# A two-layer diffusion trunk: two more weight chunks split by DMA and ScalarE, one more chunk by seven products, and sign changes tied to a place

## The chip, the cores and the metric

The kernel runs on one core of a Trainium2 chip. The core has five engines that this document names as the profile does: PE (TensorE, matmuls), DVE (VectorE), ACT (ScalarE), POOL (GpSimd) and SP (SyncE), and 16 DMA engines that serve the queues of all of them. The metric is the time of one execution on the device in microseconds; lower is better.

## The reference

Two layers work on a latent of 512 tokens with 1024 channels. Layer 0 mixes the tokens by attention, layer 1 by a Fourier transform over tokens and channel groups and a linear map. Each layer ends in a gated feed-forward network (FFN) with a convolution of width three over the tokens.

```python
def fourier_mix(h):
    hg = h.reshape(b, l, FNET_GROUPS, d // FNET_GROUPS).astype(F32)
    f = jnp.fft.fft2(hg, axes=(1, 3), norm="ortho").real

def conv_ffn(h, w_up, conv_w, conv_b, w_down):
    u = h @ w_up                                   # 512 x 1024 times 1024 x 5632
    up = jnp.pad(u, ((0, 0), (1, 1), (0, 0)))
    u = up[:, :-2] * conv_w[0] + up[:, 1:-1] * conv_w[1] + up[:, 2:] * conv_w[2] + conv_b
    gate, val = jnp.split(u, 2, axis=-1)
    return (jax.nn.silu(gate) * val) @ w_down

for i in range(DEPTH):
    h = modulate(rms_norm(x, norm_g[i, 0]), sh1, sc1)
    y = attention_mixers(...) if i % 2 == 0 else fourier_mix(h) @ w_f
    x = x + g1 * rms_norm(y, norm_g[i, 1])
    h = modulate(rms_norm(x, norm_g[i, 2]), sh2, sc2)
    x = x + g2 * rms_norm(conv_ffn(h, ...), norm_g[i, 3])
```

## The kernel before

Every large product is made of three matmuls on split numbers: a 32-bit value is a high half that TensorE takes in full and a low half that is what the high half left out. A product is high x high (line 102), low activation x high weight (103) and high activation x low weight (104). A weight thus needs a high half `wh` and a low half `wl`. The usual way (`split`, line 124): an SP DMA loads the raw weight, ACT casts it to `wh`, and DVE subtracts `wh` from the raw weight to give `wl` (both halves show as line 125). The other way (`up_weights_dma`, line 1115): a GpSimd DMA loads the weight straight into the place of the high half, converting as it goes, ACT writes the high half with its sign changed into the place of the low half (line 1121), and a second GpSimd DMA adds the raw weight to it there (line 1124). No DVE instruction is in it. In the code it is a generator in stages, and `pump(g)` lets a generator go on to its next `yield`.

The work runs in this order: modulation vectors and norms at the start, layer 0, the Fourier mixer, the FFN of layer 1 ("second FFN"). A tile scheduler sets the order on each engine's queue; the kernel binds it in places by `fence`/`held` and by dependencies without a semaphore (`add_manual_dep`, NoSync), which only fix who stands ahead of whom in one queue. Each engine works its queue in order.

At the start, `WARM` dummy matmuls (line 638) run on TensorE ahead of the first real work; the sums of the squares of the input (line 184) come next, with more dummies (line 178) between the first modulation products (line 653).

The Fourier mixer ends in an output loop over eight pieces `d` of 128 output channels. A piece's weight comes in raw (`fourier_load` for two pieces into parts of `yT`, others by SP), is turned into a sum (GpSimd, line 1555) and a difference (DVE, line 1556), is split, and is multiplied. The sums stand in `gacc` or in a part of `yT`. In the same loop the weights of the second FFN's first two chunks are made by `up_weights_dma`: four halves `xh`, `xl`, whose stages are let go at d = 1, 4 and 6.

The second FFN goes over 22 chunks `fi`; a chunk is 128 gate and 128 value channels, called its two channels here and numbered u = 2 fi + i. The first three chunks (u = 0 to 5) are begun before their input is complete: five of the six on the two halves of the tokens apart, with the modulation (`remod`, lines 235 to 240) between them. Chunks from 3 on are plain: 48 matmuls of 512 columns, two `wh`/`wl` pairs, of which there are five buffers. The chunks in `SEVEN[1]` are done by a recursive block scheme (Strassen's kind) with seven instead of eight block products: 84 matmuls of 256 columns, and sums of weight blocks (lines 1154 to 1157) that are split in turn; `seven_inputs` prepares the sums of the activations once, ahead of chunk `SUMS[1]`. A chunk's result goes through the convolution (ACT line 1251; DVE lines 1252 and 1254), Silu (ACT 1264), the product (DVE 1265) and a split into `xT` or `xh`/`xl`. The down product of an earlier group of chunks runs in small pieces between the chunks.

The names that the change touches are `WARM`, `SUMS`, `SEVEN`, `up_weights_dma`, `fourier_load`, `fourier_weights`, the output loop, and in `ffn` the choice of a plain chunk's weights:

```python
for i, w in enumerate(up_weights(l, wpair, [fi])):
    ps = mk(pps, [P, T], F32, "mm", 6)
    up_mm(ps, w, slice(0, T))
    cc.append(conv(fi, i, ps))
```

## Time and profile before

| | us |
|---|---|
| runs | 1148.01, 1144.15, 1145.98 |
| median | 1145.98 |
| profiled execution, its own time | 1146.97 |
| its span | 1145.2 |

| engine | busy us | share of the span |
|---|---|---|
| PE | 1113.8 | 97% |
| DVE | 901.1 | 79% |
| ACT | 595.3 | 52% |
| POOL | 173.0 | 15% |

The tables of the profile give times in microseconds from the start of the span. A row of a timeline is: start, duration, engine, line, operation, what it writes from what it reads, shape, count, and in brackets the time that the engine stood idle before it and what it waited for. The share of busy time is a mean over stages; what a change in one stage is worth is read from that stage.

### The profile page before, as it was taken

Reading aid. Unit: us, or ns where it says so; the run is one execution under the profiler, and the core shown is the slowest. Engines: PE = TensorE matmul, PEld = TensorE weight load, DVE = VectorE, ACT = ScalarE, POOL = GpSimd, SP = SyncE. Lnnn points to the kernel's source line nnn. Section 1 sums busy time; section 2 is a strip of 40 time slices with the busy share of each in tenths; the row PEclk is TensorE's granted clock in tenths of the full one; section 3 lists DMA queues with packets and bytes.
Section 4 is the critical chain, followed back from the end, with each engine's and each line's share of the span. In section 5 each row is a group of like instructions: output and inputs, shape, how many; then the busy total and the mean of one; then the engine's idle time right before and its main releaser. Section 6 shows DMA issues by size and latency. Waiting matters only on the chain.

```text
span 1145.2 us, 19542 instructions
## 1 busy us (share of the span) xinstructions
PE 1113.8 (97%) x7796; PEld 966.4 (84%) x7796; DVE 901.1 (79%) x1469; ACT 595.3 (52%) x1068; POOL 173.0 (15%) x180
## 2 busy tenths in 40 slices
PE   8999999999999999999999999899999999999995
PEld 5689988868898978987898898879878898899995
DVE  4678777765679976987999667878998899879755
ACT  4342356666565633552465445557746555555533
POOL 1136332521420000000000143520000000000012
PEclk9999999999999999999999999999999999999998
DMA  9676101075143355635534401822214533323332
GB/s 368 243 241 220 38 1 38 6 262 211 38 185 111 98 200 218 221 120 195 201 106 174 132 5 56 243 107 111 74 47 142 207 102 115 102 79 102 106 143 74
DMA packets 33763, 155.83 MB, mean 136 GB/s; under 512 B 3460, under 2 KB 8196, under 8 KB 22024
## 3 DMA queue, kind: packets, MB, share of 16 engines
q1 hardware_dynamic: 32520, 150.39, 37.0%
q0 software_dynamic: 1152, 4.19, 1.5%
q8 instruction: 61, 1.00, 0.4%
q14 instruction: 30, 0.25, 0.1%
HBM read 148.28 MB, written 6.29 MB: 135 GB/s over the span
## 4 chain that ended last, share of the span: by engine, by line
PE 83%; DVE 9%; ACT 3%; DMA 3%; issue 1%; POOL 1%; DVEq 0%; POOLq 0%; SPq 0%; ACTq 0%
PE mm L102 24%; PE mm L103 22%; PE mm L104 22%; DVE wl L125 2%; PE PT L950 1%; DMA raw<-in_w_up 1%; DVE md_t L302 1%; PE O L102 1%; PE gm L527 1%; PE O L103 1%; PE gm L102 1%; PE mm L178 1%; PE gm L104 1%; PE gm L103 1%; PE O L104 1%
## 5 line engine op out<-in xcount | busy, mean ns | idle before, releaser
L125 ACT CAST wh<-raw 128x1024 fp32r<-128x1024 f32 (+2 forms) x207 | 190.7, 933 | 170.5 <-PE mm L103 115.0
L125 DVE TENSOR_TENSOR wl<-raw,wh 128x1024 fp32r<-128x1024 f32 (+2 forms) x197 | 214.4, 1097 | 53.8 <-ACT wh L125 53.5
L102 PE MATMUL mm<-hh,wh 128*128 128x256 f32 (+1 forms) x632 | 206.4, 327 | 2.1 <-ACT yT L925 0.9
L104 PE MATMUL mm<-hh,wl 128*128 128x256 f32 (+1 forms) x632 | 203.6, 322 | 0.0
L103 PE MATMUL mm<-hl,wh 128*128 128x256 f32 (+1 forms) x632 | 203.5, 322 | 0.0
L277 POOL TENSOR_TENSOR gacc<-gacc,sq 128x256 f32<-128x256 f32 (+1 forms) x33 | 28.0, 848 | 716.6 <-ACT sq L275 715.7
L102 PEld LDWEIGHTS mm<-hh,wh 128*128 128x128 f32 x632 | 118.9, 188 | 18.3 <-ACT sq L1190 5.1
L103 PEld LDWEIGHTS mm<-hl,wh 128*128 128x128 f32 x632 | 118.8, 188 | 11.2
L104 PEld LDWEIGHTS mm<-hh,wl 128*128 128x128 f32 x632 | 118.9, 188 | 10.4 <-DVE wl L125 0.4
L102 PE MATMUL mm<-zh,wh 128*128 128x256 f32 x384 | 109.2, 284 | 0.7 <-ACT sq L1188 0.6
L102 PE MATMUL mm<-xh,wh 128*128 128x512 f32 (+1 forms) x302 | 107.5, 356 | 0.0
L103 PE MATMUL mm<-xl,wh 128*128 128x512 f32 (+1 forms) x302 | 106.8, 354 | 0.0
L103 PE MATMUL mm<-zl,wh 128*128 128x256 f32 x384 | 106.6, 278 | 0.0
L104 PE MATMUL mm<-zh,wl 128*128 128x256 f32 x384 | 106.5, 277 | 0.0
L104 PE MATMUL mm<-xh,wl 128*128 128x512 f32 (+1 forms) x302 | 106.2, 352 | 0.0
L102 PEld LDWEIGHTS mm<-zh,wh 128*128 128x128 f32 x384 | 72.3, 188 | 5.0 <-ACT sq L1193 3.6
L103 PEld LDWEIGHTS mm<-zl,wh 128*128 128x128 f32 x384 | 72.3, 188 | 0.0
L104 PEld LDWEIGHTS mm<-zh,wl 128*128 128x128 f32 x384 | 72.1, 188 | 0.0
L102 PEld LDWEIGHTS mm<-xh,wh 128*128 128x128 f32 x302 | 56.8, 188 | 9.9 <-issue 1.6
L103 PEld LDWEIGHTS mm<-xl,wh 128*128 128x128 f32 x302 | 56.8, 188 | 8.7 <-issue 0.4
L104 PEld LDWEIGHTS mm<-xh,wl 128*128 128x128 f32 x302 | 56.7, 188 | 8.6
L1251 ACT ACTIVATE cv<-mm,cols 128x512 f32<-128x512 f32 x59 | 45.9, 778 | 27.3 <-PE mm L104 21.6
(434 smaller groups left out, 2798.1 us busy)
## 6 DMA issues: line engine op xcount, KB each, us to landing
raw<-in_w_up SPq DMA_DIRECT2D x42, 1024.0 KB, 4.9
xT<-in_mod_r SPq DMA_DIRECT2D x20, 1024.0 KB, 4.9
raw<-in_w_down SPq DMA_DIRECT2D x32, 384.0 KB, 3.1
raw<-in_mod_p SPq DMA_DIRECT2D x8, 1024.0 KB, 4.9
raw<-in_w_down SPq DMA_DIRECT2D x16, 512.0 KB, 4.0
raw<-in_w_in SPq DMA_DIRECT2D x6, 1024.0 KB, 7.7
yT<-in_mod_r SPq DMA_DIRECT2D x10, 512.0 KB, 6.2
raw<-in_w_out SPq DMA_DIRECT2D x4, 1024.0 KB, 4.9
```

The lines of the kernel that those rows point to most:

```text
L102: i = PE.matmul(out, lhsT=ah, rhs=bh, start=start, stop=False, skip_group_check=skip)
L103: PE.matmul(out, lhsT=ah, rhs=bl, start=False, stop=False, skip_group_check=skip)
L104: return i, PE.matmul(out, lhsT=al, rhs=bh, start=False, stop=stop, skip_group_check=skip)
L125: i = S.copy(out=h, in_=src), eng.tensor_tensor(out=l, in0=src, in1=f(h), op=ALU.subtract)
L178: PE.matmul(ps[:32, :src.shape[1]], lhsT=ones32, rhs=src, start=True, stop=True)
L277: G.tensor_tensor(out=self.acc[:, sl], in0=self.acc[:, sl], in1=sq[:, sl], op=ALU.add)
L302: m = V.scalar_tensor_tensor(out=t, in0=yT[:, k, hs], scalar=der[:, l, gi, k:k + 1], in1=R, op0=ALU.mult, op1=ALU.mult)
L527: PE.matmul(ps[32 * q:32 * q + 32, :], lhsT=spad[:, k, :], rhs=w[:, q * T:(q + 1) * T], start=k == 0, stop=k == KC - 1)
L950: PE.transpose(out=pt[:, j * P:(j + 1) * P], in_=Ps[j][:, off:off + P], identity=ident)
L1251: S.activation(out=cv, in_=ps, func=AF.Identity, bias=bc, scale=wc[1])
```

## The change

1. `WARM` goes from 22 to 36.
2. In `up_weights_dma` the sign changes are let go one at a time, each bound behind the ACT instruction that was written last before it; the accumulating DMA of one follows when the next sign change is let go.
3. In the Fourier output loop those stages are let go at d = 1, 3, 4, 5, 6 and 7. The raw weights of pieces 0 and 1 go to other places of `yT` (1 to 3 and 4 to 6), and piece 1's sum to `yT` 2 to 4, so that piece 3's sum no longer shares its place.
4. In the second FFN, chunk 2's weights (`soon`) and chunk 3's (`fourth`) are made by `up_weights_dma` too. The stages of chunk 2 are let go ahead of and between the tiles of the mixer's residual (`rest`), those of chunk 3 before `pre()` and after each `remod`.
5. Chunk 7 joins the chunks that are done by seven products, and their inputs are made ahead of chunk 6.

```diff
--- before.py
+++ after.py
@@ -32,9 +32,9 @@
 
 FIRST = 3
 
-SUMS = [5, 7]
-
-SEVEN = [(5, 6, 8, 10, 12, 14, 15, 17, 18, 20), (8, 9, 10, 11, 12, 13, 14, 15, 16, 17, 18, 19, 20, 21)]
+SUMS = [5, 6]
+
+SEVEN = [(5, 6, 8, 10, 12, 14, 15, 17, 18, 20), (7, 8, 9, 10, 11, 12, 13, 14, 15, 16, 17, 18, 19, 20, 21)]
 
 
 GEMV = {0: (0, 5, 7), 1: (0, 2, 4, 6)}
@@ -50,7 +50,7 @@
 GP = [1, 1]
 BP = [4, 1]
 
-WARM = 22
+WARM = 36
 HOT = [5, 8, 5, 6]
 HOT2 = [2, 2, 2]
 
@@ -1117,11 +1117,15 @@
         for (wh, wl), src in ws:
             G.dma_start(out=wh, in_=src)
         yield
-        for (wh, wl), src in ws:
-            S.activation(out=wl, in_=f(wh), func=AF.Copy, scale=-1.0)
-        yield
-        for (wh, wl), src in ws:
-            G.dma_start(out=wl, in_=src, accum_op=ALU.add)
+        for i, ((wh, wl), src) in enumerate(ws):
+            if i:
+                G.dma_start(out=ws[i - 1][0][1], in_=ws[i - 1][1], accum_op=ALU.add)
+            last = [j.name for j in nc.cur_bb.bb.instructions if j.engine == mybir.EngineType.Activation][-1]
+            j = S.activation(out=wl, in_=f(wh), func=AF.Copy, scale=-1.0)
+            tc.add_manual_dep(j.ins, last, mybir.DependencyInfo(
+                mybir.DependencyClass.NoSync, mybir.DependencyReason.DATA), reason="order")
+            yield
+        G.dma_start(out=wl, in_=src, accum_op=ALU.add)
         yield [[(wh[:, k, :], wl[:, k, :]) for k in range(KC)] for (wh, wl), src in ws]
 
 
@@ -1328,6 +1332,8 @@
                 sweep(us, ha)
                 for u in us:
                     S.copy(out=ub[:, 0, u % 2, u // 2:u // 2 + 1], in_=first[u][3][:, HT:HT + 1])
+            fourth = up_weights_dma(l, wpair, [3])
+            pump(fourth)
             pre()
 
             taps = [cols[:, C_CW + (l * 3 + t) * 44:C_CW + (l * 3 + t + 1) * 44].rearrange(
@@ -1344,11 +1350,13 @@
             R[0] = spread(R[0], pps)
             fence()
             remod(0, *n2, R[0], eng=V)
+            pump(fourth)
             R[1] = plain.rows(1)
             sweep(range(skew), halves[1], range(*SWEEP))
             R[1] = spread(R[1], pps)
             sweep(range(skew), halves[1], range(SWEEP[1], KC))
             remod(1, *n2, R[1], eng=V)
+            pump(fourth)
             SY.dma_start(out=away, in_=xT)
             xp2 = mk(cp, [P, 2, 2, 2, T], F32R, "xT")
             places = [(xp2[:, i, 0], xp2[:, i, 1]) for i in (0, 1, 0, 1)]
@@ -1381,7 +1389,7 @@
                     cc = [conv(fi, i, u, None, i == 1) for i, u in enumerate(seven_products(l, fi, pps, bs))]
                 else:
                     cc = []
-                    for i, w in enumerate(up_weights(l, wpair, [fi])):
+                    for i, w in enumerate(next(fourth) if l and fi == 3 else up_weights(l, wpair, [fi])):
                         ps = mk(pps, [P, T], F32, "mm", 6)
                         up_mm(ps, w, slice(0, T))
                         cc.append(conv(fi, i, ps))
@@ -1543,14 +1551,14 @@
 
 
         def fourier_load(d):
-            r = yT[:, 2 * d + 2:2 * d + 4, :].rearrange("p a (g i c) -> p (a g) i c", i=2, c=P)
+            r = yT[:, 3 * d + 1:3 * d + 3, :].rearrange("p a (g i c) -> p (a g) i c", i=2, c=P)
             SY.dma_start(out=r, in_=a["w_f"][d])
             return r
 
         def fourier_weights(d, eng=G):
             r = f_first[d] if d < 2 else raw([P, 4, 2, P], a["w_f"][d])
 
-            pm = (yT[:, 6:8, :] if d in (1, 3, 5) else mk(cp, [P, 2, T], F32, "gacc")).rearrange(
+            pm = (yT[:, 6:8, :] if d in (3, 5) else yT[:, 2:4, :] if d == 1 else mk(cp, [P, 2, T], F32, "gacc")).rearrange(
                 "p a (g c) -> p a g c", g=4)
             held(eng.tensor_tensor(out=pm[:, 0, :, :], in0=r[:, :, 0, :], in1=r[:, :, 1, :], op=ALU.add))
             held(V.tensor_tensor(out=pm[:, 1, :, :], in0=r[:, :, 1, :], in1=r[:, :, 0, :], op=ALU.subtract))
@@ -1599,9 +1607,9 @@
         ys = YStat(wk, 2)
         for d in range(KC):
             wh, wl = w_f.pop() if w_f else fourier_weights(d)
-            if d in (1, 4):
+            if d in (1, 3, 4, 5, 6):
                 pump(soon)
-            elif d == 6:
+            elif d == 7:
                 early = next(soon)
             pq = mk(pps, [P, T], F32, "mm", 6)
             for g in range(4):
@@ -1622,6 +1630,8 @@
             else:
                 ys.add(pps, yT[:, d, :], [0, 1])
 
+        soon = up_weights_dma(1, wpair, [2])
+        pump(soon)
         split(hh[:, :, HT:HT + 2], hl[:, :, HT:HT + 2], n2[1].unsqueeze(2).to_broadcast([P, KC, 2]))
 
 
@@ -1630,7 +1640,11 @@
         y1 = ys
         rest = plain.tiles(y1, 0, 1, 1, pps, n2[0], True, V, True)
         pump(rest)
-        pump(rest, 5)
+        pump(rest, 3)
+        pump(soon)
+        pump(rest, 2)
+        pump(soon)
+        early += next(soon)
         fence()
         ys = ffn(1, xp, early, lambda: pump(plain.tiles(y1, 1, 1, 1, pps, n2[0], False, V, True), 6),
                  lambda y: pump(boundary(y, 0, 1, 3, pps, None, a["out"]), 100), gemv_pair(1, 5, pps, xp), plain)
```

Lines of the kernel after stand up to some 15 lines further down, and buffer numbers are others.

On ACT in the Fourier output loop, before: `A` and `qs` belong to the pieces 0 and 1, `acc` to the sums of their squares, `wh<-gacc` is piece 2's high half, `xl<-xh` are the sign changes.

```order
L125 CAST A_1052_7237<-mm_7567 128x258
L1121 ACTIVATE xl_7737<-xh_7736 128x1024
L1614 COPY qs_7723<-mm_7694 128x256
L1121 ACTIVATE xl_7739<-xh_7738 128x1024
L1618 COPY yT_68<-mm_7707 128x1
L1614 COPY qs_7777<-mm_7748 128x256
L1121 ACTIVATE xl_7741<-xh_7740 128x1024
L264 ACTIVATE acc_7728<-yT_68 128x512
L1618 COPY yT_68<-mm_7761 128x1
L125 CAST wh_7790<-gacc_7787 128x1024
L275 ACTIVATE sq_7782<-yT_68 128x512
L125 CAST wh_7835<-yT_68 128x1024
```

After:

```order
L125 CAST A_1052_7251<-mm_7581 128x258
L1622 COPY qs_7737<-mm_7708 128x256
L1626 COPY yT_68<-mm_7721 128x1
L1622 COPY qs_7791<-mm_7762 128x256
L264 ACTIVATE acc_7742<-yT_68 128x512
L125 CAST wh_7804<-gacc_7801 128x1024
L1626 COPY yT_68<-mm_7775 128x1
L125 CAST wh_7849<-yT_68 128x1024
L1124 ACTIVATE xl_7751<-xh_7750 128x1024
L275 ACTIVATE sq_7796<-yT_68 128x512
L1622 COPY qs_7837<-mm_7808 128x256
L125 CAST wh_7896<-gacc_7893 128x1024
```

The cast of piece 2's high half stands behind the first copy of the sums in both, but the three sign changes that stood ahead of it now follow piece 3's cast.

On DVE in the second FFN, chunks 3 and 4, before: `mm_8787` and `mm_8820` are chunk 3's two results, `mm_8859` and `mm_8892` chunk 4's, `wl_8889` the low half of chunk 4's second weight.

```order
L1250 TENSOR_TENSOR sq_8715<-mm_8324,Rs_8600 128x256
L1265 TENSOR_TENSOR cv_1261_8701<-cv_1259_8692,cv_1261_8701 128x512
L1252 SCALAR_TENSOR_TENSOR cv_1265_8771<-mm_8669,cols_64,cv_1265_8771 128x511
L125 TENSOR_TENSOR wl_8889<-raw_8853,wh_8888 128x1024
L125 TENSOR_TENSOR xT_8668<-cv_1261_8701,xT_8668 128x512
L1252 SCALAR_TENSOR_TENSOR cv_1263_8714<-sq_8715,cols_64,cv_1263_8714 128x511
L1254 SCALAR_TENSOR_TENSOR cv_1265_8771<-mm_8669,cols_64,cv_1265_8771 128x511
L1254 SCALAR_TENSOR_TENSOR cv_1263_8714<-sq_8715,cols_64,cv_1263_8714 128x511
L1258 TENSOR_TENSOR cv_1263_8714<-cv_1263_8714,ub_8208 128x1
```

After: `mm_8805` and `mm_8834` are chunk 3's results, `mm_8873` chunk 4's first, `wl_8903` the low half of chunk 4's second weight.

```order
L1256 SCALAR_TENSOR_TENSOR cv_1273_8859<-mm_8834,cols_64,cv_1273_8859 128x511
L1269 TENSOR_TENSOR cv_1268_8794<-cv_1266_8737,cv_1268_8794 128x512
L1258 SCALAR_TENSOR_TENSOR cv_1271_8830<-mm_8805,cols_64,cv_1271_8830 128x511
L1258 SCALAR_TENSOR_TENSOR cv_1273_8859<-mm_8834,cols_64,cv_1273_8859 128x511
L125 TENSOR_TENSOR xT_8691<-cv_1268_8794,xT_8691 128x512
L1269 TENSOR_TENSOR cv_1273_8859<-cv_1271_8830,cv_1273_8859 128x512
L1256 SCALAR_TENSOR_TENSOR cv_1278_8898<-mm_8873,cols_64,cv_1278_8898 128x511
L125 TENSOR_TENSOR wl_8903<-raw_8867,wh_8902 128x1024
L125 TENSOR_TENSOR xT_8691<-cv_1273_8859,xT_8691 128x512
```

Before, that low half stands ahead of the convolution of chunk 3's results; now it stands behind the convolution of both and behind the first step of chunk 4's own first result.

On PE at the change from chunk 4's first channel to its second, before: `wh_8855` and `wh_8888` are the chunk's two weights.

```order
L103 MATMUL mm_8859<-hl_70,wh_8855 128x512
L104 MATMUL mm_8859<-hh_69,wl_8856 128x512
L102 MATMUL mm_8892<-hh_69,wh_8888 128x512
L103 MATMUL mm_8892<-hl_70,wh_8888 128x512
L104 MATMUL mm_8892<-hh_69,wl_8889 128x512
L102 MATMUL mm_8892<-hh_69,wh_8888 128x512
```

After: `wh_8869` and `wh_8902` are chunk 4's weights, `wh_8943` and `wh_8976` chunk 5's, `wh_9035` and `wh_9068` chunk 6's.

```order
L104 MATMUL mm_8873<-hh_69,wl_8870 128x512
L102 MATMUL mm_8906<-hh_69,wh_8902 128x512
L103 MATMUL mm_8906<-hl_70,wh_8902 128x512
L102 MATMUL mm_8947<-hh_69,wh_8943 128x512
L103 MATMUL mm_8947<-hl_70,wh_8943 128x512
L102 MATMUL mm_8980<-hh_69,wh_8976 128x512
L103 MATMUL mm_8980<-hl_70,wh_8976 128x512
L102 MATMUL mm_9039<-hh_69,wh_9035 128x512
L103 MATMUL mm_9039<-hl_70,wh_9035 128x512
L102 MATMUL mm_9072<-hh_69,wh_9068 128x512
L103 MATMUL mm_9072<-hl_70,wh_9068 128x512
L104 MATMUL mm_8906<-hh_69,wl_8903 128x512
```

Before, the second weight's three products follow at once; now the two products that need only high halves of five weights stand ahead of the first product with a low half.

## Rows read from the trace of the kernel before

**Rows 1.** The page's head: busy time, its share of the span, instructions by engine.

```profile
PE 1113.8 (97%) x7796; PEld 966.4 (84%) x7796; DVE 901.1 (79%) x1469; ACT 595.3 (52%) x1068; POOL 173.0 (15%) x180
```

**Rows 2.** By stretch: window, busy of each engine (count), granted clock, DMA share, GB/s.

```profile
8.00:10.00 2.00, 1.96 (x35) 1.03 (x25) 0.87 (x5) 0.49 (x2) 0.00 (x0) 0.54 0.92 349
790.00:804.00 14.00, 13.99 (x116) 13.73 (x115) 14.00 (x35) 14.00 (x35) 0.00 (x0) 1.00 0.00 0
804.00:830.00 26.00, 26.00 (x112) 20.94 (x113) 25.05 (x50) 19.94 (x27) 0.00 (x0) 1.00 0.22 81
830.00:855.00 25.00, 25.00 (x110) 20.11 (x108) 23.94 (x28) 11.63 (x16) 0.00 (x0) 1.00 0.12 43
984.00:992.00 8.00, 8.00 (x67) 7.61 (x66) 7.30 (x11) 3.56 (x7) 0.00 (x0) 1.00 0.48 171
```

**Rows 3.** The chain that ended last, first 20 us: start, us, what.

```profile
8.88 3.33 PE mm L178 x9
14.38 2.13 PE mm L178 x9
```

**Rows 4.** TensorE's timeline at the start: start, us, instruction, count, [idle before, releaser].

```profile
1.11 4.33 PE L638 MATMUL mm<-maskb 128*128 128x256 bf16 x22 [1.11 <-DVE maskb L634]
7.31 1.57 PE L184 MATMUL mm<-sqx,ones 128*32 128x64 f32 x64 [1.86 <-ACT sqx L681]
```

**Rows 5.** TensorE's timeline, Fourier output loop.

```profile
732.03 0.38 PE L102 MATMUL mm<-B,wh 128*128 128x256 f32 x1 [1.84 <-ACT wh L125]
737.22 0.38 PE L104 MATMUL mm<-B,wl 128*128 128x256 f32 x1 [1.03 <-DVE wl L125]
```

**Rows 6.** ScalarE's timeline, Fourier output loop.

```profile
729.41 1.06 ACT L1121 ACTIVATE xl<-xh 128x1024 fp32r<-128x1024 f32 x1 [0.63 <-DMA xh<-in_w_up]
730.93 1.04 ACT L125 CAST wh<-gacc 128x1024 fp32r<-128x1024 f32 x1
```

**Rows 7.** VectorE's timeline, Fourier output loop.

```profile
732.01 1.23 DVE L125 TENSOR_TENSOR wl<-gacc,wh 128x1024 fp32r<-128x1024 f32 x1 [0.52 <-ACT wh L125]
734.86 2.31 DVE L125 TENSOR_TENSOR wl<-yT,wh 128x1024 fp32r<-128x1024 f32 x1
```

**Rows 8.** GpSimd's timeline, Fourier output loop.

```profile
734.35 1.74 POOL L1555 TENSOR_TENSOR gacc<-raw 128x512 f32<-128x512 f32 x1
736.03 0.89 POOL L1124 DMA_DIRECT2D xl<-in_w_up  x1
```

**Rows 9.** VectorE's groups by line, 790 to 860 us: busy, mean ns.

```profile
L125 DVE TENSOR_TENSOR wl<-raw,wh 128x1024 fp32r<-128x1024 f32 (+1 forms) x12 | 14.0, 1168 | 0.0
L1254 DVE SCALAR_TENSOR_TENSOR cv<-mm,cols,cv 128x511 f32<-128x511 f32 x10 | 7.3, 739 | 0.0
L1265 DVE TENSOR_TENSOR cv<-cv,cv 128x512 f32<-128x512 f32 x7 | 4.7, 678 | 0.0
```

**Rows 10.** ScalarE's timeline, second FFN.

```profile
805.64 2.94 ACT L125 CAST wh<-raw 128x1024 fp32r<-128x1024 f32 x3
```

**Rows 11.** TensorE's timeline, second FFN, where chunk 3 begins.

```profile
803.83 0.50 PE L102 MATMUL mm<-hh,wh 128*128 128x512 f32 x1
```

**Rows 12.** DMA issues, 715 to 890 us: count, KB each, us to landing.

```profile
xh<-in_w_up POOLq DMA_DIRECT2D x4, 512.0 KB, 5.6
xl<-in_w_up POOLq DMA_DIRECT2D x4, 512.0 KB, 9.2
```

**Rows 13.** DMA issues by line, the page's part.

```profile
raw<-in_w_down SPq DMA_DIRECT2D x16, 512.0 KB, 4.0
```

**Rows 14.** ScalarE's groups by line and form, 790 to 860 us.

```profile
L1251 ACT ACTIVATE cv<-mm,cols 128x512 f32<-128x512 f32 x10 | 7.8, 776 | 8.8 <-PE mm L104 7.5 <-DVE xT L125 1.3
L1264 ACT ACTIVATE cv<-cv 128x512 f32<-128x512 f32 x8 | 5.0, 629 | 3.9 <-DVE cv L1254 3.9
L125 ACT CAST xT<-cv 128x512 fp32r<-128x512 f32 x4 | 2.5, 613 | 0.0
```

**Rows 15.** TensorE's waits, 800 to 890 us: us in total, times, longest.

```profile
PE mm L102 <- ACT sq L1188: 0.6, 1, 0.6
```

## Prediction

> **What bounds the kernel now.** I read the page's head first: TensorE is busy 97% of a span of 1145.2 us, VectorE 79%, ScalarE 52% [rows 1]. What can be won is the 3% in which TensorE stands, stretches at a low clock, and matmuls that a cheaper form leaves out; what can be lost is any place where another engine delivers a weight too late. So I went to the three places that the change touches.
>
> At the start the granted clock is 0.54 from 8 to 10 us [rows 2], so that most of these 2 us went at the lower of its two levels, 1.2 GHz. The chain of waits runs through nine dummy matmuls that take 3.33 us there, and through the same nine 5 us later in 2.13 us [rows 3]. Ahead of the fall TensorE does 22 dummies from 1.11 to 5.44, then stands 1.86 us until the first squares arrive [rows 4].
>
> In the Fourier output loop TensorE waits twice: 1.84 us for a weight's high half at 732.03, and 1.03 us for a low half at 737.22 [rows 5]. The high half is a ScalarE cast at 730.93, and ScalarE comes to it late because it waited for a weight DMA until 729.41, to change a sign [rows 6]. The low halves are VectorE's: 1.23 us at 732.01, and after a difference a subtract that takes 2.31 us [rows 7].
>
> From 804 to 855 us TensorE never waits (26.00 of 26.00 us, 25.00 of 25.00), but VectorE is at 25.05 of 26 and from 790 to 804 both VectorE and ScalarE are full [rows 2]. This stretch holds chunks 3 to 7 of the second FFN, and VectorE is as near to setting its pace as TensorE.
>
> **The change, part by part.** Start. Fourteen more dummies at the full clock's spacing fill part of the 1.86 us. In rows 22 took 4.33 us, most of it cold; the last few have 0.11 each, so 36 end near 7.0, ahead of the 7.31 at which the squares' sums begin [rows 4]. If the clock then stays up at 8 us, the nine dummies and the one after them lose 3.33 - 2.13 = 1.2 us [rows 3]. Behind that stands input: the share of the DMA engines is 0.92 there [rows 2], so not all may be cashed. I take -0.9; bounds 0 and -1.2. Were the extra dummies cold throughout, 36 x 0.21 = 7.7 us would end at 8.8, and the start would lose 1.5. But the 22 of before already end fast, so I give that little weight.
>
> Fourier loop. The sign changes go to places later in the loop, and the third piece's cast stands right behind the sum's copy instead of behind three sign changes (the order of ScalarE above). The cast then starts near 728.8, 2.1 us earlier. VectorE's subtract can't follow as far: it stays behind the second piece's last difference, which needs that piece's last matmul (done by 732.03 - 1.84 = 730.19 [rows 5], and then two short steps), so it ends near 731.9 instead of 733.2 [rows 7]: 1.3. The second wait, 1.03 us, has no cause left once its low half is earlier by as much. That is 2.3; upper bound 1.84 + 1.03 = 2.9, lower 0.8 (only the first wait's part, less half a microsecond in case GpSimd's sum for the second piece, now in another place of yT, comes later). I take -2.3, since the two waits are next to each other and TensorE works without a wait for the rest of the loop.
>
> Second FFN. Chunks 2 and 3 lose four VectorE subtracts, 1.17 each [rows 9], to GpSimd DMAs and ScalarE sign changes. Chunk 7 becomes seven products of half size: 84 matmuls at 8.00/67 = 0.119 are 10.0 us, 48 of 512 columns at 26.00/112 = 0.232 are 11.1 [rows 2]; -1.1 for TensorE. For VectorE it is dearer: sums of weights and seven low halves come to about 8.3 us instead of 2.4 (by width: 1.17 for 1024 columns, 0.68 for 512 [rows 9]). So the stretch gains 4.7 us of VectorE time early and pays 5.9 late.
>
> What decides is where the subtracts stand. In the new order of VectorE the low half of chunk 4's second weight has 27 instructions between it and that of the chunk's first weight, where 13 stood before, and TensorE, in its new order, does two matmuls each of five weights ahead of the first that needs it. I worked the wait out by hand. (1) Chunk 3's first low half: ScalarE's sign change ends near 799.0 and its accumulating DMA lands near 804.2, when TensorE wants it: 0. (2) Its second: the sign change stands behind the copies of the second remod, where the cast at 805.64 is now [rows 10], ends near 806.8, and the DMA lands 5.1 us later at 811.9; TensorE starts chunk 3 at 803.83 [rows 11] and wants this half after 28 matmuls of 0.232, at 810.3: wait 1.6. The 5.1 is an estimate, with the issue in it: between the 4.0 of a plain 512 KB load [rows 13] and the 5.6 that plain DMAs from GpSimd's queue took in the full Fourier loop, above the lower since this one reads what it adds to; its upper bound is the 9.2 of the accumulating ones there [rows 12]. (3) Chunk 4's second low half: ahead of it ScalarE casts a weight whose buffer only comes free when chunk 4's first matmuls are done, at T; then 0.97 (cast), 0.53 (cast), 0.70 (conv), 0.55 (Silu) and VectorE 0.60, 0.67 and 1.15 follow one another [rows 9, 10, 14], their durations less the 0.08 by which rows overlap,, to T + 5.2. TensorE has ten matmuls, 2.3 us: wait 2.9. (4) Chunk 6's first low half: 16.5 us of VectorE work from there, 15.8 of TensorE's: 0.8. Sum 5.3; if TensorE only waited for VectorE's own work, about 2.
>
> The skill has a price for (2). The Trainium skill, "DMA: Bandwidth & Descriptors" (Anatomy of one DMA, SWDGE path), fits a GpSimd DMA by 2.0 us and its bytes at 436 GB/s, which for 512 KB is 3.2 us, an estimate from that page. The trace disagrees: the plain ones took 5.6 and the accumulating ones 9.2 [rows 12]. By that price the wait (2) would be 0 and the sum 1.6 us lower.
>
> Of the wait of 0.6 us that begins the first chunk by seven products [rows 15] half may go, -0.3. Together +5.3 - 1.1 - 0.3 = +3.9; bounds -1.4 (no wait at all) and +8.4 (the 9.2 for (2)).
>
> Sum: -0.9 - 2.3 + 3.9 = +0.7, against the profiled execution's own 1146.97 (a span of 1145.2 and 1.8 around it), 1147.7. That execution stands 1.0 over the median of the runs, 1145.98, so the median to expect is 1146.7 us. What is measurable here is 0.3%, 3.4 us. This is no change.
>
> **The rivals.** *Faster*: VectorE's queue holds no one up, since the waits (2) to (4) rest on an order in which ScalarE's cast happens to be late. For it: TensorE didn't wait once in 804 to 855 before with four subtracts more [rows 2]. Against: those subtracts stood earlier. Then the stretch gives -1.4 and the whole -4.6: 1141.4. It decides if waits (2) to (4) stay under 1.1 together (-3.5).
>
> *Slower*: the accumulating DMA is as slow as in the Fourier loop, 8.0 to 9.2 us instead of 5.1, and chunk 3's second low half arrives 2.9 to 4.1 us later than I take it; nothing on TensorE can move into the gap. For it: all four that there are [rows 12]. Against: those ran beside loads, while the DMA share from 790 to 804 is 0.00 and then 0.22 [rows 2]. That gives 1149.6 to 1150.8; it decides from a transfer of about 7.8 us. A page has a rule for it: the Trainium skill, "SBUF — State Buffer" (Who interferes with whom), has VectorE and GpSimd lock each other out of a shared port for whole instructions. The trace agrees for arithmetic: a subtract took 2.31 us instead of 1.23 beside a GpSimd sum [rows 7, 8]; GpSimd's own DMA instruction kept to 0.89 beside that subtract [rows 8], so I don't raise the chance for it.
>
> *It doesn't do what it says*: the clock falls anyway and the Fourier cast is held by something else; then only 0.8 of the 3.2 us comes and the time is 1149.1.
>
> **How the numbers follow.** My forecast 0.55, the faster rival 0.20, the slower 0.18, the third 0.07. The forecast's own range is 1143 to 1149.5, from the bounds of the start, the loop and the waits; a little of it lies on each side of the 0.3%. The range reaches to both rivals, 1141.4 to 1150.8; two in ten are left for what lies beyond their times. Faster 0.21, same 0.58, slower 0.21.
>
> **What would show it.** Right: granted clock near 1.0 from 8 to 12 us, and the first such matmuls 1 us earlier; no wait at 732; TensorE waits in 809 to 840 for an accumulating DMA and for VectorE's low halves, some 5 us in all; chunk 7 shorter by a microsecond. Wrong: TensorE busy throughout 804 to 855 (the faster rival), a first wait of over 4 us near 810 (the slower), or the fall of the clock still at 8 us.

## The result and the profile after

The changed kernel takes 1148.63 us (median of 16 runs, 1146.75 to 1152.62) against 1145.98 before (median of 15; a sixteenth execution took 2735.76 and is left out); the ratio is 1.0023 with an interval of 1.0013 to 1.0032. It is slower by some 2.6 us, clear of noise though less than the 0.3% that was called no change. The time lies 1.9 us over the forecast of 1146.7 and inside its range, 1141.4 to 1150.8. The profiled execution took 1149.96 us with a span of 1147.8, 2.6 longer than that of before.

TensorE has 50 matmul records more (14 dummies, and 36 for chunk 7) and 1.5 us less of busy time than in [rows 1]:

```profile
PE 1112.3 (97%) x7846; PEld 966.1 (84%) x7846; DVE 902.4 (79%) x1472; ACT 598.9 (52%) x1074; POOL 179.5 (16%) x188
```

**Where the time went.** I matched points of TensorE's timeline in the two traces; the difference is after less before.

| place | before | after | difference |
|---|---|---|---|
| comes to a pause in the Fourier mixer | 705.35 | 704.21 | -1.1 |
| ends the Fourier loop | 755.80 | 752.57 | -3.2 |
| begins chunk 3 of the second FFN | 803.83 | 800.42 | -3.4 |
| is through with chunk 8 | 871.41 | 872.09 | +0.7 |
| is through with chunk 10 | 914.64 | 916.40 | +1.8 |
| last matmul | 1134.21 | 1137.14 | +2.9 |

So 3.4 us were won up to chunk 3, 4.1 were lost in chunks 3 to 8, and 2.2 more behind them.

**The start** came as forecast. The dummies fill most of the pause, the squares' sums begin at 7.43 (7.31 in [rows 4]):

```profile
1.12 5.74 PE L638 MATMUL mm<-maskb 128*128 128x256 bf16 x36 [1.12 <-DVE maskb L634]
7.43 0.65 PE L184 MATMUL mm<-sqx,ones 128*32 128x64 f32 x32 [0.57 <-ACT sqx L681]
```

The table by stretch (columns as in [rows 2]) has the clock at 1.00 from 8 to 10 us, and in the Fourier mixer, where before had a second fall. First the rows of after:

```profile
8.00:10.00 2.00, 1.63 (x45) 1.07 (x38) 1.11 (x5) 1.02 (x3) 0.00 (x0) 1.00 1.04 417
711.00:715.00 4.00, 3.92 (x31) 3.87 (x32) 3.42 (x10) 2.46 (x8) 0.00 (x0) 1.00 0.18 51
795.00:870.00 75.00, 69.54 (x389) 58.95 (x388) 70.47 (x110) 48.44 (x75) 1.75 (x2) 1.00 0.24 63
870.00:930.00 60.00, 57.29 (x364) 50.70 (x363) 51.53 (x65) 32.06 (x53) 0.00 (x0) 1.00 0.51 167
```

Then those of before for the last three stretches:

```profile
711.00:715.00 4.00, 3.96 (x21) 3.76 (x19) 1.14 (x6) 1.32 (x4) 0.00 (x0) 0.57 0.02 4
795.00:870.00 75.00, 74.38 (x388) 62.64 (x388) 71.16 (x114) 49.16 (x78) 0.00 (x0) 1.00 0.18 58
870.00:930.00 60.00, 59.17 (x381) 52.80 (x380) 53.98 (x68) 34.25 (x56) 0.00 (x0) 1.00 0.52 176
```

From 795 to 870 us TensorE is idle for 5.5 of 75 us (75.00 - 69.54) where it was 0.6 before; from 870 to 930 it is 2.7 against 0.8.

**The Fourier loop.** The wait of 1.84 us at 732.03 [rows 5] is now 0.32 at 729.47. The second didn't go: two shorter ones stand in its place. And two more, of 0.30 and 0.61 us, come early in the loop, where before had none. Together TensorE waits 2.6 us in the loop, against 2.9 before.

```profile
721.42 0.39 PE L104 MATMUL mm<-B,wl 128*128 128x256 f32 x1 [0.61 <-DVE wl L125]
729.47 0.39 PE L102 MATMUL mm<-B,wh 128*128 128x256 f32 x1 [0.32 <-ACT wh L125]
736.78 0.39 PE L104 MATMUL mm<-B,wl 128*128 128x256 f32 x1 [0.76 <-DVE wl L125]
741.27 0.39 PE L104 MATMUL mm<-B,wl 128*128 128x256 f32 x1 [0.60 <-DVE wl L125]
```

What was won in the mixer was won ahead of the loop. The matmul that stands at 715.31 before stands at 711.78 after, 3.5 us earlier; at the loop's end the lead is 3.2. By the traces, a sum on GpSimd lies behind this. Before, it ran beside VectorE's work for the mixer, where an instruction took 1.60 us that took 0.47 in after, and TensorE then waited 1.55 us (at 710.69, the row stands further down), with a fall of the clock behind it:

```profile
707.62 1.28 POOL L1555 TENSOR_TENSOR yT<-yT 128x512 f32<-128x512 f32 x1
707.58 1.60 DVE L360 SCALAR_TENSOR_TENSOR hl<-xT,der,hh 128x256 fp32r<-128x256 f32 x1
```

After, the first sums stand at 716.31 and 718.02, beside the subtracts for the first two pieces, which take 1.64 and 1.84 us instead of 1.22 and 1.20. The two new waits follow from these:

```profile
718.02 2.27 POOL L1563 TENSOR_TENSOR yT<-raw 128x512 f32<-128x512 f32 x1
719.53 1.84 DVE L125 TENSOR_TENSOR wl<-yT,wh 128x1024 fp32r<-128x1024 f32 x1
```

**The second FFN.** TensorE's four waits, in the places that the hand schedule gave:

```profile
801.88 0.49 PE L104 MATMUL mm<-hh,wl 128*128 128x512 f32 x1 [0.83 <-DMA wl<-in_w_up]
809.41 0.51 PE L104 MATMUL mm<-hh,wl 128*128 128x512 f32 x1 [1.20 <-DMA wl<-in_w_up]
825.09 0.50 PE L104 MATMUL mm<-hh,wl 128*128 128x512 f32 x1 [2.81 <-DVE wl L125]
841.53 0.51 PE L104 MATMUL mm<-hh,wl 128*128 128x512 f32 x1 [0.54 <-DVE wl L125]
```

ScalarE's two sign changes of chunk 3, and the cast that waits for the buffer of chunk 4's first weight:

```profile
794.74 1.05 ACT L1124 ACTIVATE wl<-wh 128x1024 fp32r<-128x1024 f32 x1
802.42 1.05 ACT L1124 ACTIVATE wl<-wh 128x1024 fp32r<-128x1024 f32 x1
819.75 1.05 ACT L125 CAST wh<-raw 128x1024 fp32r<-128x1024 f32 x1 [2.88 <-PE mm L103]
```

GpSimd issues the two accumulating DMAs 0.4 us behind the sign changes' ends:

```profile
796.22 0.87 POOL L1122 DMA_DIRECT2D wl<-in_w_up  x1 [27.13 <-ACT hh L236]
803.89 0.88 POOL L1128 DMA_DIRECT2D wl<-in_w_up  x1 [6.80 <-ACT wl L1124]
```

and they land after 5.6 us (columns as in [rows 12]):

```profile
wl<-in_w_up POOLq DMA_DIRECT2D x2, 512.0 KB, 5.6
```

VectorE's low half of chunk 4's second weight, behind the first convolution step of that chunk's first result; TensorE goes on at 825.09, right behind its end:

```profile
823.16 0.74 DVE L1256 SCALAR_TENSOR_TENSOR cv<-mm,cols,cv 128x511 f32<-128x511 f32 x1
823.82 1.22 DVE L125 TENSOR_TENSOR wl<-raw,wh 128x1024 fp32r<-128x1024 f32 x1
```

**Behind 870 us** there are three waits that the prediction didn't have:

```profile
912.60 0.39 PE L102 MATMUL mm<-zh,wh 128*128 128x256 f32 x1 [1.22 <-ACT sq L1197]
924.41 0.39 PE L102 MATMUL mm<-zh,wh 128*128 128x256 f32 x1 [0.80 <-ACT sq L1192]
926.47 0.39 PE L104 MATMUL mm<-hh,wl 128*128 128x256 f32 x1 [0.62 <-DVE wl L125]
```

The first is held by a copy on ScalarE, which stands in its queue behind a cast that waited for a weight's load:

```profile
911.66 0.62 ACT L125 CAST wh<-raw 128x512 fp32r<-128x512 f32 x1 [3.41 <-DMA raw<-in_w_up]
```

That load waits, on SP's queue, for VectorE to free its buffer, and VectorE was late since it had stood 1.63 us for another DMA, of the modulation's weights:

```profile
893.91 1.28 DVE L458 SCALAR_TENSOR_TENSOR gacc<-xl,scol,gacc 128x1024 f32<-128x1024 f32 x1 [1.63 <-DMA xl<-in_mod_r]
```

### The profile page after: what moved, and what is told of

It is laid out like the page before. It is cut to its first block, busy times and chain, and to the rows that moved or that the text cites. A ratio compares the mean times of both kernels' runs of the same rounds, so it can differ in the third digit from the quotient of the medians.

```text
span 1147.8 us, 19662 instructions
## 1 busy us (share of the span) xinstructions
PE 1112.3 (97%) x7846; PEld 966.1 (84%) x7846; DVE 902.4 (79%) x1472; ACT 598.9 (52%) x1074; POOL 179.5 (16%) x188
## 4 chain that ended last, share of the span: by engine, by line
PE 78%; DVE 12%; ACT 4%; DMA 2%; issue 2%; POOL 1%; SPq 0%; DVEq 0%; POOLq 0%; ACTq 0%
PE mm L102 22%; PE mm L104 21%; PE mm L103 21%; DVE wl L125 2%; PE PT L950 1%; DMA xl<-in_mod_r 1%; DVE md_t L302 1%; PE O L102 1%; PE gm L527 1%; PE O L103 1%; PE gm L102 1%; PE gm L104 1%; PE gm L103 1%; DMA raw<-in_w_kva 1%; PE O L104 1%
## 5 line engine op out<-in xcount | busy, mean ns | idle before, releaser
L125 DVE TENSOR_TENSOR wl<-raw,wh 128x1024 fp32r<-128x1024 f32 (+2 forms) x195 | 211.6, 1094 | 53.8 <-ACT wh L125 53.4
L104 PE MATMUL mm<-hh,wl 128*128 128x256 f32 (+1 forms) x628 | 200.3, 320 | 6.0 <-DVE wl L125 4.0
L102 PE MATMUL mm<-hh,wh 128*128 128x256 f32 (+1 forms) x628 | 203.5, 324 | 1.3 <-ACT yT L925 0.9
L103 PE MATMUL mm<-hl,wh 128*128 128x256 f32 (+1 forms) x628 | 200.7, 320 | 0.0
L102 PE MATMUL mm<-zh,wh 128*128 128x256 f32 x400 | 113.6, 284 | 2.0 <-ACT sq L1197 1.2
L103 PE MATMUL mm<-zl,wh 128*128 128x256 f32 x400 | 111.0, 278 | 0.0
L104 PE MATMUL mm<-zh,wl 128*128 128x256 f32 x400 | 110.9, 277 | 0.0
L102 PEld LDWEIGHTS mm<-zh,wh 128*128 128x128 f32 x400 | 75.2, 188 | 6.5 <-ACT sq L1197 4.9
L103 PEld LDWEIGHTS mm<-zl,wh 128*128 128x128 f32 x400 | 75.3, 188 | 0.0
L104 PEld LDWEIGHTS mm<-zh,wl 128*128 128x128 f32 x400 | 75.1, 188 | 0.0
```

The costliest lines, as they stand in the source:

```text
L102: i = PE.matmul(out, lhsT=ah, rhs=bh, start=start, stop=False, skip_group_check=skip)
L103: PE.matmul(out, lhsT=ah, rhs=bl, start=False, stop=False, skip_group_check=skip)
L104: return i, PE.matmul(out, lhsT=al, rhs=bh, start=False, stop=stop, skip_group_check=skip)
L125: i = S.copy(out=h, in_=src), eng.tensor_tensor(out=l, in0=src, in1=f(h), op=ALU.subtract)
```

## The experiments

The theories as they stood at first: (1) the loss comes with chunk 3's weights, by late DMAs and by the order that follows; (2) VectorE has too little time, since seven products at chunk 7 cost it 5.9 us more. Every ratio below is to the kernel before from the same chip, whose median is given.

**Start and Fourier loop alone.** Against the changed kernel:

```diff
-SUMS = [5, 6]
+SUMS = [5, 7]
-... (7, 8, 9, 10, ...
+... (8, 9, 10, ...
-        soon = up_weights_dma(1, wpair, [2])
-            fourth = up_weights_dma(l, wpair, [3])
...
```

> The start (36 dummies) and the Fourier loop with the sign changes let go one by one, nothing else: second FFN as before. My theory (the gains of start and loop are real and stay; the loss is made in the second FFN): 3.2 us less than before, ratio 0.9972, granted clock 1.0 from 8 to 12 us, no wait of TensorE over 0.5 us in the Fourier loop. Rival (what is won in front is given back later, since later loads and waits do not move along): under 1.5 us less, with new waits behind 880 us.

Measured: 1143.51 us against 1146.36, ratio 0.9971 (0.9960 to 0.9983). The gains are real and most of them last; the time lies 2.85 us below before. The waits in the Fourier loop are those of after, up to 0.76 us, not under 0.5. Behind 880 us one wait of 0.70 us stands at 907, with the second FFN as before.

**Chunk 3's weights by the old way.** In the changed kernel:

```diff
-            fourth = up_weights_dma(l, wpair, [3])
-            pump(fourth)
...
-                    for i, w in enumerate(next(fourth) if l and fi == 3 else up_weights(l, wpair, [fi])):
+                    for i, w in enumerate(up_weights(l, wpair, [fi])):
```

> The changed kernel, but chunk 3's weights by the old way (SP load, ScalarE cast, VectorE subtract). Theory 1 (the loss comes with chunk 3's weights: two waits for accumulating DMAs, 2.0 us, and the low half of chunk 4's second weight that stands behind the convolutions, 2.8): TensorE waits under 1 us in 800 to 845, 3 to 4 us less than before, ratio 0.997. Theory 2 (VectorE has too little time, because chunk 7 by seven products costs it 5.9 us and here nothing is taken off it from chunk 3 on): waits for low halves of 4 us and more in 820 to 860, no faster than before.

Measured: 1154.57 against 1146.36, ratio 1.0069 (1.0054 to 1.0084). Theory 1 alone is out: it had 3 to 4 us less than before, and the time is some 8 us more, and 5.3 more than the changed kernel's by the ratios. TensorE's waits from 800 to 875 have become one, and the clock falls in and behind it, to 0.51 from 840 to 850:

```profile
845.06 0.79 PE L104 MATMUL mm<-hh,wl 128*128 128x512 f32 x1 [9.39 <-DVE wl L125]
```

**Chunk 7 plain.** In the changed kernel:

```diff
-SUMS = [5, 6]
+SUMS = [5, 7]
-... (7, 8, 9, 10, ...
+... (8, 9, 10, ...
```

> The changed kernel, but chunk 7 with plain products and the inputs of the seven products made where they were. Theory 1 (chunk 3's weights): the waits of 0.8, 1.2 and 2.8 us in 800 to 826 stay, the one of 0.5 at 841 may go; 0.5 to 1.5 us more than the changed kernel less that wait, so within 1 us of it, ratio to before about 1.002. Theory 2 (VectorE's work for chunk 7): the wait of 2.8 goes, and it is 2 to 3 us faster than before, ratio 0.998.

Measured: 1149.02 against 1146.36, ratio 1.0025 (1.0015 to 1.0035); the changed kernel had 1.0023. The first three waits stay within 0.2 us (4.9 in all), and the fourth is gone:

```profile
801.57 0.50 PE L104 MATMUL mm<-hh,wl 128*128 128x512 f32 x1 [1.04 <-DMA wl<-in_w_up]
808.94 0.50 PE L104 MATMUL mm<-hh,wl 128*128 128x512 f32 x1 [1.04 <-DMA wl<-in_w_up]
824.62 0.50 PE L104 MATMUL mm<-hh,wl 128*128 128x512 f32 x1 [2.81 <-DVE wl L125]
```

So theory 2 alone is out as well. Each of the two edits brings a loss of its own, and the two losses don't add: 5.5 us for the weights of chunks 2 and 3 (1149.02 - 1143.51), 12.7 for chunk 7 (next run, 1159.03 - 1146.36), 5.5 for both (2.65 over before in the changed kernel, 2.85 below it with start and Fourier loop alone).

**Chunk 7 by seven products alone.** In the kernel before:

```diff
-SUMS = [5, 7]
+SUMS = [5, 6]
-... (8, 9, 10, ...
+... (7, 8, 9, 10, ...
```

> The kernel before with chunk 7 by seven products, inputs made ahead of chunk 6, and nothing else. Theory 1: TensorE's work falls by 1.1 us and waits of 0.5 to 1 us come at 840, net 0 to -1 us, ratio 0.9995. Theory 2: VectorE's 5.9 us more end in TensorE waits of 3 us and more, ratio 1.002 or above.

Measured: 1159.03 against 1146.36, ratio 1.0108 (1.0092 to 1.0125), far beyond both. One wait of 9.39 us:

```profile
847.89 0.80 PE L104 MATMUL mm<-hh,wl 128*128 128x512 f32 x1 [9.39 <-DVE wl L125]
```

VectorE has that low half behind the low halves `zl` of the seven products' inputs:

```profile
844.35 2.36 DVE L125 TENSOR_TENSOR zl<-yT,zh 128x1024 fp32r<-128x1024 f32 x2
846.62 2.36 DVE L125 TENSOR_TENSOR wl<-raw,wh 128x1024 fp32r<-128x1024 f32 x2
```

and TensorE's clock falls in and behind the wait, which takes more (the granted clock is the third column from the right; it is 0.70 in the ten microseconds that are nearly all wait, and 0.90 behind them):

```profile
838.00:848.00 10.00, 0.61 (x5) 0.36 (x3) 9.58 (x11) 3.94 (x5) 0.00 (x0) 0.70 0.00 0
848.00:870.00 22.00, 22.00 (x124) 19.23 (x125) 16.79 (x20) 10.38 (x14) 0.00 (x0) 0.90 0.18 61
```

This gave theory 3: a low half costs what its place in VectorE's queue costs. Theory 2 has VectorE at 9.58 of 10 us there, and 6.0 us more of VectorE's busy time in the whole trace (907.1 against 901.1), so it speaks for itself too.

**Chunk 3's stages one step earlier.** In the changed kernel:

```diff
             pump(fourth)
             pre()
+            pump(fourth)
...
             remod(1, *n2, R[1], eng=V)
-            pump(fourth)
```

> The changed kernel, but the two sign changes of chunk 3's weights are let go one step earlier each (behind the norm's last tile and behind the first remod), so that the accumulating DMAs start some 8 us sooner. That also changes the order the scheduler finds: the low halves of chunks 4 and 5 stand early again, those of chunk 6 stand behind the inputs of the seven products as where chunk 7 was changed alone. Theory 3 (a low half costs what its place in VectorE's queue costs: behind the inputs of the seven products and convolutions that wait for TensorE it is late by a round trip): the waits of 0.8, 1.2 and 2.8 us in 800 to 826 go, and one of 8 to 10 us comes near 830 to 840; 4 to 6 us slower than the changed kernel, ratio to before about 1.006. Rival (VectorE's time, no matter in which order): its work is the same, so the waits together stay near 5 us and the time near 1148.6; or, if the late sign changes were all there is, 1144.

Measured: 1149.63 against 1146.37, ratio 1.0028 (1.0018 to 1.0037). The waits up to 826 are gone, as theory 3 has it; the new one is 5.51 us, less than it asked for, and as much as the four of the changed kernel together, which is what theory 2 has. Ahead of it VectorE is busy for 38.59 of 39 us:

```profile
840.27 0.80 PE L104 MATMUL mm<-hh,wl 128*128 128x512 f32 x1 [5.51 <-DVE wl L125]
```

```profile
795.00:834.00 39.00, 39.00 (x189) 32.34 (x188) 38.59 (x71) 30.19 (x47) 0.88 (x1) 1.00 0.16 41
```

**Chunk 6's weights ahead of the inputs, too.** Against the last:

```diff
                 if fi == SUMS[l]:
+                    w6 = list(up_weights(l, wpair, [6])) if l else None
                     bs = seven_inputs(xp)
...
+                    ... w6 if l and fi == 6 else up_weights(l, wpair, [fi])):
```

> As the run with the stages earlier, and the weights of chunk 6 are written ahead of the inputs of the seven products, so that chunk 6's low halves no longer stand behind them. Theory 3 (the place in the queue): no wait over 1.5 us up to 845; what VectorE lacks shows at chunk 7, 0 to 3 us; 1142.5 to 1145.5, ratio about 0.998. Rival (VectorE's time): waits of 5 us or more altogether, only at another chunk, 1147 or above.

Measured: 1148.47 against 1146.37, ratio 1.0016 (1.0006 to 1.0025). Theory 3 asked for 1145.5 at most and missed; the rival, VectorE's time, had 1147 or above. TensorE works through up to 846, and then waits at chunk 7 for 4.0 us, the same lack at a later place:

```profile
PE mm L104 <- DVE wl L125: 2.4, 1, 2.4
PE mm L102 <- ACT wh L125: 1.6, 1, 1.6
```

**The same without any of chunk 2's and 3's DMAs.** Start, Fourier loop, chunk 7 by seven products, chunk 6's weights first:

> Start and Fourier loop as changed, chunk 7 by seven products, chunks 2 and 3 by the old way, the weights of chunk 6 written ahead of the inputs. Against the run of chunk 7 alone (wait of 9.4 us at one low half): Theory 3 (place in the queue) says that wait goes, and what is left is the time that VectorE lacks: its 5.9 us more, less the 4.3 us that it stood idle in 804 to 872 before, 1 to 3 us of waits at chunk 7 and 1.1 us of TensorE's work saved; 1143.5 to 1146. Rival (VectorE's time in whatever order): a wait of 8 us or more stays, 1152 or above.

Measured: 1150.28 against 1146.37, ratio 1.0039 (1.0025 to 1.0053), outside what either theory gave. The 9.4 us of chunk 7 alone become 5.29, at chunk 7's first product with new weights. So the place did matter, for some 4 us; the rest stayed, more than the 1 to 3 that I gave it:

```profile
851.76 0.58 PE L102 MATMUL mm<-zh,wh 128*128 128x256 f32 x1 [5.29 <-ACT wh L125]
```

**Less work for VectorE.** As the run with chunk 6's weights first, but without four subtracts; the high halves stand in for the low halves of the inputs' sums, so the second FFN's output is another:

```diff
-            split(*b[n], src)
+            if bare:
+                held(S.copy(out=b[n][0], in_=src))
+                b[n] = (b[n][0], b[n][0])
+            else:
+                split(*b[n], src)
```

> As the run with the stages earlier and chunk 6's weights first, but in the second FFN the four subtracts that make the low halves of the sums of the seven products' inputs are left out (4 x 1.13 us of VectorE; the high halves stand in their place, so the output is another). All else, TensorE's products too, is the same. Theory (VectorE's time is the bound of 795 to 870 once chunk 7 is done by seven products): the waits of 2.4 and 1.6 us near 846 and 851 fall by 3 to 4 us, to under 1 us, and the time by 3 to 4.5, to 1144 to 1145.5. Rival (order only: a low half or a weight that stands behind a convolution waits for TensorE's round trip whatever VectorE has to do): waits stay near 4 us, 1148.

Measured: 1142.01 against 1147.06, ratio 0.9957 (0.9944 to 0.9970). Against its counterpart's ratio of 1.0016 that is 0.6%, 6.8 us, more than the 3 to 4.5 that I asked for. The waits are gone to the last:

```profile
795.00:870.00 75.00, 75.00 (x425) 64.72 (x424) 71.28 (x114) 52.12 (x82) 0.88 (x1) 1.00 0.25 71
```

4.5 us of VectorE's work less took 4.0 us of waits away: in this stretch VectorE's time was the bound, once the queue's order no longer was. Of the other 2.8 us about half is the lower clock behind the waits (0.98 on average in its counterpart's 795 to 870, 1.00 here, which makes 1.5 us of 75). The two traces show where the other half went: in the counterpart's the clock fell in the Fourier loop too, to 0.81 and 0.77 from 720 to 728, which took 1.5 us; here it didn't. That has nothing to do with the four subtracts, which are worth some 5.5 us.

**Earlier stages, chunk 7 plain.** In the changed kernel, chunk 3's stages one step earlier as above, and `SUMS` and `SEVEN` as before:

> The changed kernel with chunk 3's stages let go earlier and chunk 7 plain: chunks 2 and 3 by DMA and ScalarE, and no more work for VectorE. Theory (the 5 us of waits in the run without seven products at chunk 7 came from the late stages of chunk 3 and the order that follows from them): no wait over 0.5 us from 795 to 850, the time of the run with start and Fourier loop alone, 1143.5, within 0.7 us; VectorE's spared 4.7 us are worth nothing there. Rival (the DMA way itself costs, by its traffic or by ScalarE's two more passes): 1146 or above with other waits.

Measured: 1142.50 against 1147.06, ratio 0.9959 (0.9946 to 0.9971). The DMA way costs nothing when its stages are let go in time. TensorE stands for 0.15 us in all from 790 to 1000:

```profile
795.00:870.00 75.00, 74.99 (x388) 63.18 (x387) 70.02 (x111) 48.59 (x75) 0.88 (x1) 1.00 0.23 68
870.00:930.00 60.00, 59.93 (x380) 53.22 (x380) 54.66 (x69) 35.05 (x55) 0.00 (x0) 1.00 0.48 165
```

It is faster than before, and than the changed kernel. Whether it also beats start and Fourier loop alone (0.9971) is not settled, as the intervals overlap. Against the run with the stages earlier (1.0028), which differs by chunk 7 alone, it shows what seven products there cost once chunk 3's waits are out: 0.7%, some 8 us.

In its Fourier loop the waits are as in the changed kernel, none over 0.61 us ahead of 724, and yet the clock fell:

```profile
720.00:724.00 4.00, 3.39 (x17) 2.98 (x17) 4.00 (x7) 0.00 (x0) 4.00 (x5) 0.70 0.73 225
```

**Chunk 4's weights by DMA as well**, in the run with chunk 6's weights first:

> As the run with the stages earlier and chunk 6's weights first, and chunk 4's two weights by DMA and ScalarE as well: two VectorE subtracts (2 x 1.15 us) fewer ahead of the place where TensorE waits. Theory (VectorE's time is the bound there): the waits of 4.0 us near 846 and 851 fall by about 2.3 us, to 1.5 to 2, and the time by 2 to 3.5 against that run, to 1145 to 1146.5: still above the run without seven products at chunk 7 (1142.5). Rival (the order, or chunk 4's late buffer): waits stay at 4 us or come earlier, near 820, 1148 or above.

Measured: 1147.44 against 1146.87, ratio 1.0004 (0.9993 to 1.0015). The waits at 846 and 851 are gone altogether, but chunk 4's second weight comes late: ScalarE gets to its sign change at 821.16, and the accumulating DMA is issued at 822.62. 3.2 us of waits stand at 820 to 828 instead, the longest for this DMA:

```profile
PE mm L104 <- DMA wl<-in_w_up: 2.1, 1, 2.1
```

So I missed on the time by 1 us, and on the place. That 2.3 us of subtracts less took 4.0 us of waits away doesn't speak for VectorE's time here, as the earlier waits held TensorE for 3.2 us meanwhile.

**The dummies alone.**

```diff
-WARM = 22
+WARM = 36
```

> The kernel before with 36 instead of 22 dummies at the start. Theory: granted clock 1.0 from 8 to 12 us, the nine dummies of 3.33 us take 2.1, and all later work is 0.9 us earlier: ratio 0.9992. Rival: what is won at the start is given back at the next wait for input, ratio 1.0000, and the start of layer 0's products as before.

Measured: 1145.96 against 1146.37, ratio 0.9995 (0.9986 to 1.0004): not to be told from nothing, nor from the 0.9 us. In its trace the clock is 1.00 from 8 to 10 us, and at 704 us TensorE is 1.4 us earlier than before. The Fourier loop gave it back in this execution. The wait that before had at 732.03 stands at 730.27, and behind it the clock fell, to 0.59 and 0.56, with 16 and 22 matmul records in 4 us where a full stretch has 32:

```profile
730.27 0.39 PE L102 MATMUL mm<-B,wh 128*128 128x256 f32 x1 [1.72 <-ACT wh L125]
```

```profile
730.00:734.00 4.00, 3.73 (x16) 3.36 (x17) 3.71 (x3) 2.64 (x4) 3.16 (x2) 0.59 1.03 247
734.00:738.00 4.00, 4.00 (x22) 4.00 (x22) 3.96 (x3) 2.03 (x3) 3.65 (x4) 0.56 1.03 245
```

**The Fourier loop alone**, with 22 dummies:

> The kernel before with the Fourier loop as changed and the 22 dummies. Theory: 2.3 us less than before, ratio 0.998, no wait at 732, and TensorE's clock 1.0 all through 705 to 760; with the 0.4 that the dummies alone gave this falls short of the 2.9 of both, the rest being a stretch at the lower clock that moves with the phase of the waits in the loop. Rival: 2.9 us less, the dummies count for nothing.

Measured: 1145.11 against 1147.06, ratio 0.9985 (0.9976 to 0.9994), 1.7 us. The clock falls at 8 us as before (0.50 from 8 to 10). It isn't 1.0 all through the mixer either, as I had it: it stays up at 711 to 715, and falls behind the new wait of 0.61 us at 722:

```profile
724.00:728.00 4.00, 4.00 (x23) 3.87 (x21) 2.69 (x5) 0.53 (x2) 1.98 (x1) 0.57 1.04 328
```

The two parts alone give 0.4 and 1.7, together 2.9; with intervals of about 1 us each that is no proof that they help each other. Falls of the clock that come in one trace and not in the next, as here and in the rows at 730, take more than the 0.8 us that is missing.

## Why the prediction held, point by point

**Start, -0.9.** The trace has -1.1 at 704 us, with the clock as forecast. Right in place and size; what it is worth by itself in the final time is open (0.4 with an interval from -0.5 to 1.6). One reason shows in the traces: with 36 dummies the clock stayed at 1.00 at 8 us in all eleven, but with 22 it didn't always fall. In the trace of chunk 7 alone it was 1.00 from 8 to 12 us, behind a wait of 1.22 us, and TensorE came to the pause at 704 2.1 us earlier than in before's. The forecast took a fall that comes in some executions for one that comes in each.

**Fourier loop, -2.3.** From 704 to the loop's end after gains 2.1 (3.2 - 1.1), and the loop alone 1.7. The number held by luck. The mechanism was right for the first wait, 1.84 to 0.32. It was wrong for the second: I let it go with the first, and it came back as 0.76 and 0.60 at later pieces, whose low halves VectorE makes beside GpSimd's sums. With the new 0.30 and 0.61 the loop's own waits fell by 0.3 us, where I had 2.3. What I didn't count made up for it, ahead of the loop: the wait of 1.55 us fell to 0.47, and the fall of the clock to 0.57 behind it didn't come, 2.4 us together. Both came with the Fourier edits, since the run of the dummies alone still has a wait of 1.54 there; that GpSimd's sum is the cause is read from the rows above, and no run moved it by itself. The row of before:

```profile
710.69 0.39 PE L102 MATMUL misc<-wh,hh 128*128 128x256 f32 x1 [1.55 <-DVE Z L125]
```

**The four waits from chunk 3 on, 0 + 1.6 + 2.9 + 0.8 = 5.3.** Measured 0.83, 1.20, 2.81 and 0.54, 5.4 in all. The two DMAs landed 6.0 us behind the sign changes, where I had 5.1 with a range of 4.0 to 9.2; the 0.9 more shows in the first wait, and what TensorE stood there it didn't stand again at the second. The order as printed, and durations from rows, were enough for this. The upper bound of the stretch is a slip: with 9.2 for 5.1 it is 3.9 + 4.1 = 8.0, not 8.4. The 0.6 us of wait of which I let half go [rows 15] went whole. The price by the Trainium skill, "DMA: Bandwidth & Descriptors" (Anatomy of one DMA, SWDGE path), 3.2 us for 512 KB, would have left the second wait out; this case's 5.6 us speaks against using it for an accumulating DMA.

**Chunk 7, -1.1.** Here the step failed though the sum didn't. TensorE's saving was there: across chunk 7 the run without four subtracts gains 1.0 us on the one with chunk 7 plain and earlier stages, and neither waits there. But alone this edit costs 12.7 us. I had written down VectorE's 5.9 us and put their price at the 0.8 us of wait (4), counted from the end of wait (3), when the waits (1) to (3) had already held TensorE for 4.5 us by my sum (4.8 measured) and VectorE had caught up. Take those waits away, and the lack appears elsewhere (5.5 us of wait with the stages earlier, some 8 us of time). I read a price off a schedule in which another loss hid it. That the remaining loss is VectorE's time is shown by the run without four subtracts; that up to 4 us more come from the place in its queue is shown by the runs with chunk 6's weights first.

**The whole, +0.7.** 2.6 were measured. The missing 1.9 are the waits at 912 to 926, which I didn't look for: chunks 9 to 11 had no edit, but their loads and queues move with VectorE. The trace shows the chain, from a DMA to VectorE, SP, a load and ScalarE; no run tested it by itself. The run with chunk 7 plain and earlier stages has no wait there, but that with start and Fourier loop alone has 0.70 us at the same place, without any edit in the second FFN. So the cause of these waits stays open in part.

**The rivals.** The slower one (a DMA of 7.8 us and more) didn't come: the transfer took 5.6 in a quiet stretch. The faster one failed since the order held TensorE as printed: the waits (2) to (4) came to 4.6 us, where it needed under 1.1. The third didn't come either, with the clock at 1.00 at 8 us and the Fourier cast's wait at 0.32.

## What to carry to other kernels

Taking work off one engine pays only where that engine is the last to deliver, and the way in which it is taken off must start early enough: here the same two DMAs cost 5.5 us or nothing, by one step of where their sign changes were let go, and the order that the scheduler then found. When two edits change the same engine's load, price each with the other's waits taken out; a hand schedule that holds TensorE up in one place makes the next place look free. A cheaper product for the bound engine is dear when the engine next to it is at 25 of 26 us.

## What the runs showed of the hardware

A wait can cost more than its length. Behind idle times of TensorE of 1.5 to 1.9 us the granted clock sometimes fell for some microseconds (0.57 at 711 to 715 in before, 0.59 and 0.56 at 730 to 738 with the dummies alone) and sometimes not (1.00 behind the 1.84 us at 732 in before, [rows 5]); with 9.4 us of idle it was 0.70 and then 0.90 up to 870. The length of one wait doesn't decide it. In the Fourier loop as changed, where no wait ahead of 724 is over 0.61 us, the clock stayed at 1.00 from 720 to 728 in the trace of start and Fourier loop alone and in that of the changed kernel, and fell to 0.70 and 0.88 in that of earlier stages with chunk 7 plain, with the same code up to there; such a fall took some 1.5 us (read from two traces, with and without it).

A VectorE instruction beside a GpSimd sum took 1.60 us instead of 0.47 (at 707.58 in before), and a subtract 1.84 instead of 1.20 (at 719.53 in after).

An accumulating DMA of 512 KB from GpSimd's queue took 5.6 us where little else moved (90 GB/s in all from 796 to 802, about what it brings itself), and 9.2 in the full Fourier loop [rows 12].
